# Low parts of the weights, the stages of sums, and the first norm's squares in another order: a decoder block on one core

## The chip, the core and the metric

One core of a Trainium2 chip runs the whole kernel. The metric is device microseconds of one execution, the median of repeated runs. In profiles the engines are PE (TensorE's matmuls), PEld (its weight loads), DVE (VectorE), ACT (ScalarE), POOL (GpSimd) and SP (SyncE, which here only issues the weights' loads and the stores of the result).

## The reference

A decoder block for 256 tokens of width 2048, one layer, all in float32:

```python
x = x + 0.5 * swiglu(rms_norm(x, ffn1_norm_g[l]), ffn1_w_gate[l], ffn1_w_up[l], ffn1_w_down[l])
h = rms_norm(x, mix_norm_g[l])
z = h @ w_in[l]
...
merged = jax.nn.sigmoid(gate_a) * attn_branch + jax.nn.sigmoid(gate_c) * conv_branch
x = x + merged @ w_out[l]
x = x + 0.5 * swiglu(rms_norm(x, ffn2_norm_g[l]), ffn2_w_gate[l], ffn2_w_up[l], ffn2_w_down[l])
return rms_norm(x, final_norm_g)
```

`swiglu` is `(silu(h @ w_gate) * (h @ w_up)) @ w_down` with 5632 columns between. Attention (8 heads, differential) and a causal convolution of width 31 over 1024 channels stand between the two feed-forward parts. The change touches how the matrix products are fed and emptied, and the mean of squares in the first `rms_norm`; what is computed stays the same.

## The kernel before

**Products in two parts.** Each float32 operand is the sum of a high part (rounded to the matmul's format, `wh` for a weight, the first 256 columns of `h`) and a low part (`wl`, the last 256 columns). A product is high x high, high x low and low x high. In `lin` (line 312) the weights stand still in TensorE: a *high* matmul streams the 512 columns of h against `wh`, a *low* one 256 columns against `wl`. A call of `lin` makes 512 columns of the result in four PSUM banks, one for each column tile; there are five such banks in the pool. It runs over units of four row tiles of 128 (`KU`), four units for 2048 rows. A unit has 16 high and 16 low matmuls, in the order high, low, or low, high in the odd units and the last one.

**Weights.** Class `Weights` (line 43) brings units of 1 MB from HBM, on SP's queue, into three raw buffers. ACT rounds a half of a unit (two row tiles, `KH`) to `wh` (`high_to`, line 89; L94), DVE subtracts to get `wl` (`low_to`, line 97; L103). There are six buffers for high halves and four for low ones; a raw buffer is loaded anew once its second low half is made. `next` (line 110) hands out a half, and first issues the high and low parts up to six and four halves ahead.

**The order of the work.** Every engine takes its instructions in the order in which the program issues them. There is no scheduler: `lin` calls `tick` (line 314) after a column tile of high matmuls or two of low ones, and each tick moves every open *flow* and the *side* jobs on. A flow is the emptying of one column tile (`evac`), a generator in stages. `halves_sum` (line 389) has ACT copy one half of the bank (rh, L392) and DVE add the other (L394). A gate product's sums go on to a product with rstd (L404), a silu on ACT (L406) and a product on POOL (L407); an up product's to a product with the gate (L424) and a split into high and low parts (L261 on ACT, L263 on DVE). `tick` takes the flows from the oldest to the newest.

**The first product.** x and the first weights arrive in pieces. For the first three units `lin` goes half by half (`halves`, line 329): `before` splits the next two tiles of x into parts of h (`split_x`, line 457; L256 on ACT, L258 on DVE), then `W.next(early=False)` issues low parts up to four halves ahead. `split_x` also squares its two tiles on POOL and adds them to `acc1` (L273, L275). After the first product `gate_late` runs `rstd_steps` in side ticks: a matmul with ones for the mean (L296), then a reciprocal root. The gate's sums wait for it in SBUF.

Of the kernel before, what the change touches and what calls it, by code (L numbers as in the profile page):

```python
# [9 lines left out]
F32 = mybir.dt.float32  # L10
F32R = mybir.dt.float32r
AF = mybir.ActivationFunctionType
ALU = mybir.AluOpType
AX = mybir.AxisListType

P = 128
T = 256
D = 2048
# [7 lines left out]
KU = 4  # L26
KH = 2
# [14 lines left out]
class Weights:  # L42
# [54 lines left out]
    def low_to(self, n):  # L97
        while self.nlow < min(n, len(self.units) * KU // KH):
# [6 lines left out]
            if k + KH == KU:  # L105
                del self.raw[u]
                self.load_to(u + 1 + self.raw_bufs)

    def next(self, held=0, early=True):


        i = self.i

        def ahead(bufs):
            n = i + bufs - held
            if self.extra and n > min(self.extra) and i <= max(self.extra):
                n = min(n + len(self.extra), max(self.extra) + 1 + bufs)
            return n

        if early:  # L120
            self.high_to(ahead(self.high_bufs))
        self.low_to(ahead(self.low_bufs))
        self.i += 1
        return self.highs.pop(i), self.lows.pop(i)

# [30 lines left out]
def block_kernel(  # L156
# [5 lines left out]
    nc = tc.nc  # L162

    const = ctx.enter_context(tc.tile_pool(name="const", bufs=1))
    big = ctx.enter_context(tc.tile_pool(name="big", bufs=1))
# [48 lines left out]
    W = Weights(nc, wpool, units, moving)  # L214
# [5 lines left out]
    xT = big.tile([P, KT, T], F32, name="xT")  # L220
# [44 lines left out]
    def tmp():  # L265
        return work.tile([P, T], F32, name="t", tag="t", bufs=5)

    def add_square(acc, src, first, square=None):
        dst = acc if first else tmp()
        if square is None:  # L270
            nc.scalar.activation(dst, src, AF.Square)
        else:
            square.tensor_tensor(dst, src, src, ALU.mult)  # L273
        if not first:
            nc.gpsimd.tensor_tensor(acc, acc, dst, ALU.add)  # L275

    def rsqrt(dst, src, scale, eps):

        shape = list(dst.shape)
        v = work.tile(shape, F32, name="rs_v", tag=f"rsv{shape[-1]}", bufs=1)  # L280
        t = tmp()[:, 0:shape[-1]]
        nc.vector.tensor_scalar(v, src, scale, eps, ALU.mult, ALU.add)
        nc.scalar.activation(dst, v, AF.Sqrt)
        yield
        nc.vector.reciprocal(dst, dst)
        yield
        nc.vector.tensor_tensor(t, dst, dst, ALU.mult)
        nc.vector.tensor_tensor(t, t, v, ALU.mult)
        yield
        nc.vector.tensor_scalar(t, t, -0.5, 1.5, ALU.mult, ALU.add)  # L290
        nc.vector.tensor_tensor(dst, dst, t, ALU.mult)
        yield

    def mean_d(acc):
        ps = pmisc.tile([P, CK], F32, name="ps_mean", tag="misc")
        nc.tensor.matmul(ps[:, 0:T], lhsT=ones, rhs=acc, start=True, stop=True)  # L296
        return ps[:, 0:T]
# [6 lines left out]
    def rstd_steps(acc, rstd, n, eps):  # L304
        yield from rsqrt(rstd, mean_d(acc), D / n, eps)
# [5 lines left out]
    side = Side()  # L311
    flows = []

    def tick(n=1):

        for f in list(flows):
            if next(f, flows) is flows:
                flows.remove(f)
        side.tick(n)

    def lin(nk, xs, evac, before=None):

        ps = [psum.tile([P, CK], F32, name="ps_mm", tag="mm") for _ in range(4)]
        nu = nk // KU

        def high(ct, parts, kt, i):
            w = parts[i // KH][0][:, i % KH, ct * P:(ct + 1) * P]  # L330
            nc.tensor.matmul(ps[ct], lhsT=w, rhs=xs(kt + i), start=(kt + i == 0), stop=(kt + i == nk - 1))  # L331

        def low(ct, parts, kt, i):
            w = parts[i // KH][1][:, i % KH, ct * P:(ct + 1) * P]
            nc.tensor.matmul(ps[ct][:, T:2 * T], lhsT=w, rhs=xs(kt + i)[:, 0:T], start=False, stop=False)  # L335

        def halves(u):

            for h in range(KU // KH):
                before(u * (KU // KH) + h)  # L340
                parts = [W.next(early=False)]
                for i in range(KH):
                    for ct in range(4):
                        high(ct, parts, u * KU + h * KH, i)
                for ct in range(4):
                    for i in range(KH):
                        low(ct, parts, u * KU + h * KH, i)
                tick(4)

        for u in range(nu):  # L350
            last = u == nu - 1
            if before is not None and not last:
                halves(u)
                continue
            parts = []
            for h in range(KU // KH):
                if before is not None:
                    before(u * (KU // KH) + h)
                parts.append(W.next(held=h))
            for product in ((low, high) if last or u % 2 == 1 else (high, low)):  # L360
                for ct in range(4):
                    for i in range(KU):
                        product(ct, parts, u * KU, i)
                    if product is high:
                        if last:
                            flows.append(evac(ct, ps[ct]))
                        tick(1.4)
                    elif ct % 2 == 1:
                        tick(1.2)
# [20 lines left out]
    def halves_sum(dst, ps, scale=1.0):  # L390
        r = work.tile([P, T], F32, name="rh", tag="rh", bufs=3)
        nc.scalar.activation(r, ps[:, T:2 * T], AF.Copy, scale=scale)  # L392
        if scale == 1.0:
            nc.vector.tensor_tensor(dst, ps[:, 0:T], r, ALU.add)  # L394
        else:
            nc.vector.scalar_tensor_tensor(dst, ps[:, 0:T], scale, r, ALU.mult, ALU.add)

    def ffn_up(h, rstd, grp, a, before=None, late=None):
        s_2 = None

        def pair_of(ci, s_t):
            def gate_act(ct):
                s = s_t[:, ct, :]
                nc.vector.tensor_tensor(s, s, rstd, ALU.mult)  # L404
                yield
                nc.scalar.activation(s, s, AF.Silu)  # L406
                nc.gpsimd.tensor_tensor(s, s, rstd, ALU.mult)  # L407

            def gate_evac(ct, ps):
                halves_sum(s_t[:, ct, :], ps)  # L410
                if late is None or ci > 0:
                    yield from gate_act(ct)
                else:
                    yield

            def gate_late():
                yield from late
                for ct in range(4):
                    yield from gate_act(ct)

            def up_evac(ct, ps):
                t = tmp()
                halves_sum(t, ps)
                nc.vector.tensor_tensor(t, t, s_t[:, ct, :], ALU.mult)  # L424
                yield
                yield from split(a(ci * 4 + ct), t)

            lin(KT, h, gate_evac, before if ci == 0 else None)
            if late is not None and ci == 0:
                side.add(gate_late(), 0.5)  # L430
            lin(KT, h, up_evac)

        for ci in range(len(grp)):
            if ci % 2 == 0:
                s_2 = big.tile([P, 2, 4, T], F32, name="s_t", tag="y")
            pair_of(ci, s_2[:, ci % 2])
# [19 lines left out]
    h1 = split_pair("P", "h1_")  # L456
    acc1, rstd1 = norm_tiles("1")

    def split_x(kt):

        fs = [split_scaled(h1(kt + k), xT[:, kt + k, :], g1_sb[:, kt + k:kt + k + 1]) for k in range(2)]
        for f in fs:
            next(f)
        for f in fs:
            next(f, None)
        for k in range(2):
            add_square(acc1, xT[:, kt + k, :], kt + k == 0, square=nc.gpsimd)

    def start(u):
        if u == 0:  # L470
            W.ahead = 1
            split_x(0)
            W.split_first()
        if u < 7:
            split_x(2 * u + 2)
        else:
            W.ahead = 3

    loads = {}

# [50 lines left out]
    for gi, grp in enumerate(groups):  # L531
        a = split_pair("Q", "a1_")
        if gi == 0:
            ffn_up(h1, rstd1, grp, a, start, rstd_steps(acc1, rstd1, D, 1e-6))
        else:
            ffn_up(h1, rstd1, grp, a)
        last = None
        if gi == len(groups) - 1:
            hm = split_pair("P", "hm_")
            accm, rstdm = norm_tiles("m")  # L540
            last = next_norm(hm, accm, loads["gm"])
        for dc in range(4):
            lin(len(grp) * 4, a, residual_evac(dc, 0.5, last))
# [376 lines left out]
    for gi, grp in enumerate(groups):  # L920
        a = split_pair("P", "a2_")
# [28 lines left out]
    for tt in range(2):  # L950
        v, y, r = ms[:, tt:tt + 1], yf[:, tt:tt + 1], rf[:, tt:tt + 1]
        for n, (c0, c1) in enumerate(((0, 512), (512, 1024), (1024, 1536), (1536, 1792), (1792, 2048))):
# [13 lines left out]
            sq = work.tile([P, CK], F32, name="sqf", tag="s2", bufs=1)  # L966
# [64 lines left out]
```

## Time and profile before

| | us |
|---|---|
| median of 3 runs (2100.57 to 2101.76) | 2100.95 |
| the profiled execution | 2100.18 |
| its span | 2098.4 |
| TensorE busy in the span | 2065.3 |

The span is the time between the first and the last instruction of the profiled execution; what lies around it is 1.8 us. A matmul's end is modelled, since matmuls overlap, so TensorE's idle time as the profile counts it begins a little late, and its rate is better read from the starts of blocks of matmuls in the chain.

### The profile page before, as it was taken

The page shows a single profiled execution, that of the slowest core. Times are in us where ns is not written, and L with a number is a line of the kernel's source. Part 1 is how long each engine was busy: PE and PEld are TensorE (multiplying, and loading weights), DVE is VectorE, ACT ScalarE, POOL GpSimd, SP SyncE. Part 2 cuts the span into 40 slices and gives each one's busy share as a digit, 9 for nine tenths or more (in the row PEclk, how much of TensorE's full clock was granted, in tenths as well). Part 3 has the DMA queues.
Part 4 walks back from the last instruction along what each step waited for, and adds up shares of the span by engine and source line. Part 5 has one row for each costly group of instructions (what it writes and reads, how often), then busy time and mean ns, then how long its engine had stood idle before and what let it go on. Part 6 is the DMA issues. An engine that isn't in the chain of part 4 may idle for free.

```text
span 2098.4 us, 28546 instructions
## 1 busy us (share of the span) xinstructions
PE 2065.3 (98%) x11230; PEld 1775.8 (85%) x11230; DVE 1375.9 (66%) x1915; ACT 1004.8 (48%) x1456; POOL 190.6 (9%) x227
## 2 busy tenths in 40 slices
PE   7999999999999999999999999999999999999998
PEld 6888888888888888888778888888888888888887
DVE  8565555665565785889888666665655655645565
ACT  6454344443344554445555744554443444434443
POOL 6201012110010110000000000100100001000011
PEclk9999999999999999999999999999999999999999
DMA  6645555566545545555545555554455555554553
GB/s 241 197 171 212 188 177 206 189 216 218 181 180 202 193 174 201 181 187 186 183 166 180 198 181 181 198 203 180 168 214 183 184 195 181 201 193 168 203 198 121
DMA packets 57735, 397.54 MB, mean 189 GB/s; under 512 B 6888, under 2 KB 6992, under 8 KB 10752
## 3 DMA queue, kind: packets, MB, share of 16 engines
q1 hardware_dynamic: 55872, 390.10, 52.2%
q0 software_dynamic: 1728, 5.61, 0.9%
q8 instruction: 88, 1.44, 0.3%
q14 instruction: 47, 0.39, 0.1%
HBM read 392.00 MB, written 3.68 MB: 189 GB/s over the span
## 4 chain that ended last, share of the span: by engine, by line
PE 88%; DVE 7%; ACT 2%; DMA 1%; issue 1%; SPq 0%; DVEq 0%; ACTq 0%
PE ps_mm L331 40%; PE ps_mm L335 21%; PE ps_mm L375 9%; PE ps_mm L376 9%; PE ps_mm L377 9%; DVE wl L103 3%; DVE t L394 2%; DVE t L424 1%; ACT rh L392 1%; DMA w<-in_ffn_w_gate_dram 1%; ACT a L261 1%; DMA w<-in_ffn_w_down_dram 1%; PE ps_s L718 0%; PE ps_o L763 0%; PE ps_tr L907 0%
## 5 line engine op out<-in xcount | busy, mean ns | idle before, releaser
L103 DVE TENSOR_TENSOR wl<-w,wh 128x1024 fp32r<-128x1024 f32 x731 | 883.3, 1248 | 484.2 <-ACT wh L94 239.9
L94 ACT ACTIVATE wh<-w 128x1024 fp32r<-128x1024 f32 x731 | 742.8, 1053 | 704.0 <-PE ps_mm L331 377.5
L331 PE MATMUL ps_mm<-h,wh 128*128 128x512 f32 x2816 | 665.2, 392 | 10.8 <-DVE h L258 10.8
L331 PEld LDWEIGHTS ps_mm<-h,wh 128*128 128x128 f32 x2816 | 523.0, 189 | 117.4 <-ACT wh L84 6.2
L335 PEld LDWEIGHTS ps_mm<-h,wl 128*128 128x128 f32 x2816 | 340.9, 188 | 25.4 <-DVE wl L103 18.1
L335 PE MATMUL ps_mm<-h,wl 128*128 128x256 f32 x2816 | 349.8, 279 | 11.2 <-DVE wl L103 11.2
L407 POOL TENSOR_TENSOR s_t<-s_t,rstd 128x256 f32<-128x256 f32 x88 | 82.7, 940 | 1158.8 <-ACT s_t L406 1158.8
L331 PE MATMUL ps_mm<-a,wh 128*128 128x512 f32 x704 | 164.9, 390 | 0.4 <-DVE t L394 0.4
L331 PEld LDWEIGHTS ps_mm<-a,wh 128*128 128x128 f32 x704 | 130.4, 188 | 26.9 <-DVE t L394 0.8
L392 ACT ACTIVATE rh<-ps_mm 128x256 f32<-128x256 f32 x208 | 77.3, 372 | 153.7 <-PE ps_mm L331 153.7
L375 PE MATMUL ps_mm<-wl,a 128*128 128x512 f32 (+1 forms) x344 | 133.1, 387 | 0.0
L377 PE MATMUL ps_mm<-wh,a 128*128 128x512 f32 (+1 forms) x344 | 132.1, 384 | 0.0
L376 PE MATMUL ps_mm<-wh,a 128*128 128x512 f32 (+1 forms) x344 | 131.9, 384 | 0.0
L375 PE MATMUL ps_mm<-wl,hm 128*128 128x512 f32 x320 | 129.8, 406 | 0.0
L377 PE MATMUL ps_mm<-wh,hm 128*128 128x512 f32 x320 | 125.1, 391 | 0.0
L376 PE MATMUL ps_mm<-wh,hm 128*128 128x512 f32 x320 | 124.9, 390 | 0.0
L331 PE MATMUL ps_mm<-hm,wh 128*128 128x512 f32 x512 | 121.0, 392 | 0.0
L331 PEld LDWEIGHTS ps_mm<-hm,wh 128*128 128x128 f32 x512 | 94.7, 188 | 19.1
L619 DVE SCALAR_TENSOR_TENSOR y_sb<-u_sb,cw_sb,y_sb 128x256 f32<-128x256 f32 x240 | 105.0, 478 | 0.0
L394 DVE TENSOR_TENSOR t<-ps_mm,rh 128x256 f32<-128x256 f32 x112 | 47.5, 424 | 63.1 <-ACT rh L392 62.9
L335 PEld LDWEIGHTS ps_mm<-a,wl 128*128 128x128 f32 x704 | 84.5, 188 | 4.5 <-DVE wl L103 2.7
L335 PE MATMUL ps_mm<-a,wl 128*128 128x256 f32 x704 | 85.6, 278 | 1.9 <-DVE wl L103 1.9
(194 smaller groups left out, 1708.2 us busy)
## 6 DMA issues: line engine op xcount, KB each, us to landing
w<-in_ffn_w_up_dram SPq DMA_DIRECT2D x88, 1024.0 KB, 4.9
w<-in_ffn_w_down_dram SPq DMA_DIRECT2D x88, 1024.0 KB, 4.9
w<-in_ffn_w_gate_dram SPq DMA_DIRECT2D x85, 1024.0 KB, 4.9
w<-in_w_in_dram SPq DMA_DIRECT2D x72, 1024.0 KB, 4.8
w<-in_w_out_dram SPq DMA_DIRECT2D x16, 1024.0 KB, 4.9
w<-in_w_attn_branch_dram SPq DMA_DIRECT2D x8, 1024.0 KB, 4.8
w<-in_w_conv_branch_dram SPq DMA_DIRECT2D x8, 1024.0 KB, 4.8
w<-in_ffn_w_gate_dram SPq DMA_DIRECT2D x5, 512.0 KB, 8.5
```

The costliest lines, as they stand in the source:

```text
L94: self.nc.scalar.activation(wh, self.raw[u][:, k:k + KH], AF.Copy)
L103: self.nc.vector.tensor_tensor(wl, self.raw[u][:, k:k + KH], self.highs[h].bitcast(F32), ALU.subtract)
L261: nc.scalar.activation(dst[:, 0:T], src, AF.Copy)
L331: nc.tensor.matmul(ps[ct], lhsT=w, rhs=xs(kt + i), start=(kt + i == 0), stop=(kt + i == nk - 1))
L335: nc.tensor.matmul(ps[ct][:, T:2 * T], lhsT=w, rhs=xs(kt + i)[:, 0:T], start=False, stop=False)
L375: nc.tensor.matmul(ps, lhsT=hi, rhs=wl[:, kk, :], start=(first and kk == 0), stop=False)
L376: nc.tensor.matmul(ps, lhsT=hi, rhs=wh[:, kk, :], start=False, stop=False)
L377: nc.tensor.matmul(ps, lhsT=lo, rhs=wh[:, kk, :], start=False, stop=(last and kk == KH - 1))
L392: nc.scalar.activation(r, ps[:, T:2 * T], AF.Copy, scale=scale)
L394: nc.vector.tensor_tensor(dst, ps[:, 0:T], r, ALU.add)
L407: nc.gpsimd.tensor_tensor(s, s, rstd, ALU.mult)
L619: nc.vector.scalar_tensor_tensor(y, src, w, y, ALU.mult, ALU.add)
```

## The change

Four edits. (1) In the last and the odd units, where the low matmuls come first, `more_lows` issues one further low half before the unit's high matmuls and a second one before the third of their four column tiles, where `next` issued both at the start of the following unit. (2) `tick` takes the flows from the newest to the oldest. (3) In the first product's halves the low parts run two halves ahead in place of four (and with them the high parts that they need). (4) The squares leave POOL: a side job `squares`, from the 27th tick on, squares four tiles at a time on ACT and adds them up on DVE; the mean waits for it (`rstd_first`). `W.ahead` was set but never read.

```diff
--- before.py
+++ after.py
@@ -106,6 +106,10 @@
                 del self.raw[u]
                 self.load_to(u + 1 + self.raw_bufs)
 
+    def more_lows(self, n):
+
+        self.low_to(self.i + self.low_bufs - KU // KH + n)
+
     def next(self, held=0, early=True):
 
 
@@ -119,7 +123,9 @@
 
         if early:
             self.high_to(ahead(self.high_bufs))
-        self.low_to(ahead(self.low_bufs))
+            self.low_to(ahead(self.low_bufs))
+        else:
+            self.low_to(i + 2)
         self.i += 1
         return self.highs.pop(i), self.lows.pop(i)
 
@@ -313,7 +319,8 @@
 
     def tick(n=1):
 
-        for f in list(flows):
+
+        for f in flows[::-1]:
             if next(f, flows) is flows:
                 flows.remove(f)
         side.tick(n)
@@ -357,8 +364,13 @@
                 if before is not None:
                     before(u * (KU // KH) + h)
                 parts.append(W.next(held=h))
-            for product in ((low, high) if last or u % 2 == 1 else (high, low)):
+            order = (low, high) if last or u % 2 == 1 else (high, low)
+            for product in order:
+                if product is high and order[0] is low:
+                    W.more_lows(1)
                 for ct in range(4):
+                    if product is high and order[0] is low and ct == 2:
+                        W.more_lows(2)
                     for i in range(KU):
                         product(ct, parts, u * KU, i)
                     if product is high:
@@ -463,18 +475,38 @@
             next(f)
         for f in fs:
             next(f, None)
-        for k in range(2):
-            add_square(acc1, xT[:, kt + k, :], kt + k == 0, square=nc.gpsimd)
 
     def start(u):
         if u == 0:
-            W.ahead = 1
             split_x(0)
             W.split_first()
         if u < 7:
             split_x(2 * u + 2)
-        else:
-            W.ahead = 3
+
+    squared = []
+
+    def squares():
+
+        sq = big.tile([P, 4, 4 * T], F32, name="sq", tag="sgc")
+        for i in range(4):
+            nc.scalar.activation(sq[:, i].rearrange("p (k t) -> p k t", k=4), xT[:, 4 * i:4 * i + 4, :], AF.Square)
+            yield
+            if i % 2 == 1:
+                nc.vector.tensor_tensor(sq[:, i - 1], sq[:, i - 1], sq[:, i], ALU.add)
+                yield
+        nc.vector.tensor_tensor(sq[:, 0], sq[:, 0], sq[:, 2], ALU.add)
+        yield
+        nc.vector.tensor_tensor(sq[:, 0, 0:2 * T], sq[:, 0, 0:2 * T], sq[:, 0, 2 * T:4 * T], ALU.add)
+        yield
+        nc.vector.tensor_tensor(acc1, sq[:, 0, 0:T], sq[:, 0, T:2 * T], ALU.add)
+        squared.append(True)
+
+    def rstd_first():
+        while not squared:
+            yield
+        yield from rstd_steps(acc1, rstd1, D, 1e-6)
+
+    side.add(squares(), 1.0, delay=26)
 
     loads = {}
 
@@ -531,7 +563,7 @@
     for gi, grp in enumerate(groups):
         a = split_pair("Q", "a1_")
         if gi == 0:
-            ffn_up(h1, rstd1, grp, a, start, rstd_steps(acc1, rstd1, D, 1e-6))
+            ffn_up(h1, rstd1, grp, a, start, rstd_first())
         else:
             ffn_up(h1, rstd1, grp, a)
         last = None
```

The order shows it in three places. The first is DVE at the end of a gate product, the second one of the kernel (s_t holds the gate's sums; wl is a low half). Before:

```order
L103 TENSOR_TENSOR wl<-w,wh 128x1024 x6
L394 TENSOR_TENSOR s_t<-ps_mm,rh 128x256
L404 TENSOR_TENSOR s_t<-s_t,rstd_113 128x256
L394 TENSOR_TENSOR s_t<-ps_mm,rh 128x256
L404 TENSOR_TENSOR s_t<-s_t,rstd_113 128x256
L394 TENSOR_TENSOR s_t<-ps_mm,rh 128x256
L404 TENSOR_TENSOR s_t<-s_t,rstd_113 128x256
L394 TENSOR_TENSOR s_t<-ps_mm,rh 128x256
L404 TENSOR_TENSOR s_t<-s_t,rstd_113 128x256
L103 TENSOR_TENSOR wl<-w,wh 128x1024 x8
```

With the change (lines shift by 12 here):

```order
L103 TENSOR_TENSOR wl<-w,wh 128x1024 x7
L406 TENSOR_TENSOR s_t<-ps_mm,rh 128x256
L416 TENSOR_TENSOR s_t<-s_t,rstd_113 128x256
L406 TENSOR_TENSOR s_t<-ps_mm,rh 128x256
L416 TENSOR_TENSOR s_t<-s_t,rstd_113 128x256
L103 TENSOR_TENSOR wl<-w,wh 128x1024
L406 TENSOR_TENSOR s_t<-ps_mm,rh 128x256
L416 TENSOR_TENSOR s_t<-s_t,rstd_113 128x256
L406 TENSOR_TENSOR s_t<-ps_mm,rh 128x256
L416 TENSOR_TENSOR s_t<-s_t,rstd_113 128x256
L103 TENSOR_TENSOR wl<-w,wh 128x1024 x7
```

One of the low halves that stood behind the four sums now stands ahead of the first, one ahead of the third.

The second is DVE in the first product (h are the parts of x, sq the squares, acc their sum). Before:

```order
L258 SCALAR_TENSOR_TENSOR h_0_110<-xT,g_sb,h_0_110 128x256 x2
L103 TENSOR_TENSOR wl<-w,wh 128x1024 x3
L258 SCALAR_TENSOR_TENSOR h_0_110<-xT,g_sb,h_0_110 128x256 x2
L103 TENSOR_TENSOR wl<-w,wh 128x1024
...
L103 TENSOR_TENSOR wl<-w,wh 128x1024
L394 TENSOR_TENSOR s_t<-ps_mm,rh 128x256 x4
L103 TENSOR_TENSOR wl<-w,wh 128x1024 x2
L282 TENSOR_SCALAR rs_v<-ps_mean 128x256
```

With the change:

```order
L264 SCALAR_TENSOR_TENSOR h_0_110<-xT,g_sb,h_0_110 128x256 x2
L103 TENSOR_TENSOR wl<-w,wh 128x1024
L264 SCALAR_TENSOR_TENSOR h_0_110<-xT,g_sb,h_0_110 128x256 x2
L103 TENSOR_TENSOR wl<-w,wh 128x1024
...
L406 TENSOR_TENSOR s_t<-ps_mm,rh 128x256 x2
L495 TENSOR_TENSOR sq<-sq 128x1024
L103 TENSOR_TENSOR wl<-w,wh 128x1024
L406 TENSOR_TENSOR s_t<-ps_mm,rh 128x256 x2
L495 TENSOR_TENSOR sq<-sq 128x1024
L497 TENSOR_TENSOR sq<-sq 128x1024
L499 TENSOR_TENSOR sq<-sq 128x512
L501 TENSOR_TENSOR acc_112<-sq 128x256
```

The h parts of the third half no longer stand behind three low halves, and the additions of the squares, with a low half among them, now stand between the first product's sums and the mean. On TensorE the matmul for the mean moves from 8 to 12 high matmuls into the second product. The third place is ACT, from the end of an up product (rh and the split into `a`) on. Before:

```order
L392 ACTIVATE rh<-ps_mm 128x256
L261 ACTIVATE a_0_116<-t 128x256
L392 ACTIVATE rh<-ps_mm 128x256
L261 ACTIVATE a_0_116<-t 128x256
L392 ACTIVATE rh<-ps_mm 128x256
L261 ACTIVATE a_0_116<-t 128x256
L392 ACTIVATE rh<-ps_mm 128x256
L94 ACTIVATE wh<-w 128x1024 x2
L261 ACTIVATE a_0_116<-t 128x256
```

With the change:

```order
L404 ACTIVATE rh<-ps_mm 128x256 x2
L267 ACTIVATE a_0_116<-t 128x256
L404 ACTIVATE rh<-ps_mm 128x256
L267 ACTIVATE a_0_116<-t 128x256
L404 ACTIVATE rh<-ps_mm 128x256
L267 ACTIVATE a_0_116<-t 128x256
L94 ACTIVATE wh<-w 128x1024 x2
L267 ACTIVATE a_0_116<-t 128x256
```

Each rh now stands ahead of the split of the tile before it. SP's order is the same as before; POOL's loses the 31 operations on squares, and nothing else of it moves against TensorE's work.

## Rows read from the trace of the kernel before

**Rows 1.** The page, busy time of each engine over the whole span.
```profile
PE 2065.3 (98%) x11230; PEld 1775.8 (85%) x11230; DVE 1375.9 (66%) x1915; ACT 1004.8 (48%) x1456; POOL 190.6 (9%) x227
```

**Rows 2.** Waits of TensorE, whole span: us in total, times, longest.
```profile
PE ps_mm L335 <- DVE wl L103: 13.9, 41, 0.6
PE ps_mm L331 <- DVE h L258: 10.8, 4, 5.8
PE ps_mm L331 <- DVE t L394: 0.4, 1, 0.4
```

**Rows 3.** The chain in order of time: start us, us, what.
```profile
39.75 0.43 PE ps_mean L296 x2
...
42.03 3.63 PE ps_mm L335 x32
...
68.34 7.28 PE ps_mm L331 x32
...
158.40 7.28 PE ps_mm L331 x32
...
225.28 7.28 PE ps_mm L331 x32
...
247.15 7.28 PE ps_mm L331 x32
```

**Rows 4.** Timeline at an up product's end: start us, us, instruction, [idle before].
```profile
56.43 7.44 PE L331 MATMUL ps_mm<-h,wh 128*128 128x512 f32 x32
...
61.46 0.42 DVE L394 TENSOR_TENSOR t<-ps_mm,rh 128x256 f32<-128x256 f32 x1 [0.42 <-ACT rh L392]
...
63.70 0.42 DVE L424 TENSOR_TENSOR t<-t,s_t 128x256 f32<-128x256 f32 x1
63.71 2.23 PE L335 MATMUL ps_mm<-h,wl 128*128 128x256 f32 x18
64.04 2.35 DVE L103 TENSOR_TENSOR wl<-w,wh 128x1024 fp32r<-128x1024 f32 x2
...
66.45 1.90 PE L335 MATMUL ps_mm<-h,wl 128*128 128x256 f32 x14 [0.51 <-DVE wl L103]
```

**Rows 5.** Timeline of the first product.
```profile
12.10 1.06 ACT L94 ACTIVATE wh<-w 128x1024 fp32r<-128x1024 f32 x1 [2.19 <-DMA w<-in_ffn_w_gate_dram]
...
16.75 1.69 DVE L258 SCALAR_TENSOR_TENSOR h<-xT,g_sb,h 128x256 fp32r<-128x256 f32 x2
...
17.63 3.78 PE L331 MATMUL ps_mm<-h,wh 128*128 128x512 f32 x8 [4.46 <-DVE h L258]
...
21.56 1.06 ACT L94 ACTIVATE wh<-w 128x1024 fp32r<-128x1024 f32 x1 [1.97 <-DMA w<-in_ffn_w_gate_dram]
...
34.69 5.06 PE L331 MATMUL ps_mm<-h,wh 128*128 128x512 f32 x21 [0.25 <-DVE h L258]
```

**Rows 6.** Windows: stretch, length, PE, PEld, DVE, ACT, POOL busy, PEclk, DMA, GB/s.
```profile
17.63:22.85 5.22, 5.22 (x16) 4.45 (x17) 5.22 (x5) 3.25 (x6) 5.06 (x6) 0.51 0.92 388
22.86:25.80 2.94, 2.94 (x19) 2.62 (x18) 2.94 (x4) 2.94 (x6) 2.78 (x4) 1.00 0.49 137
```

**Rows 7.** Durations of single kinds of instruction: by source line, timeline, costliest groups.
```profile
L258 DVE SCALAR_TENSOR_TENSOR hm<-xT,gm_sb,hm x16: 473/480/962, 703.5 to 758.7; 128x256 fp32r<-128x256 f32 x16
...
L645 ACT ACTIVATE u_sb<-y_sb x2: 1042/1044/1046, 1158.0 to 1158.9; 128x1024 f32<-128x1024 f32 x2
...
1160.01 1.23 DVE L624 TENSOR_TENSOR u_sb<-u_sb 128x1024 f32<-128x1024 f32 x1 [3.99 <-ACT u_sb L645]
...
1162.28 0.68 DVE L626 TENSOR_TENSOR u_sb<-u_sb 128x512 f32<-128x512 f32 x1
...
26.03 0.89 ACT L256 ACTIVATE h<-xT,g_sb 128x256 fp32r<-128x256 f32 x2
...
28.05 1.76 DVE L103 TENSOR_TENSOR wl<-w,wh 128x1024 fp32r<-128x1024 f32 x1
...
L619 DVE SCALAR_TENSOR_TENSOR y_sb<-u_sb,cw_sb,y_sb 128x256 f32<-128x256 f32 x240 | 105.0, 478 | 0.0
```

## The prediction

> **What bounds the kernel now.** I read the page's busy line first: TensorE is busy 98% of 2098.4 us, no other engine over 66% [rows 1]. So an edit on another engine pays only where TensorE waits for it. The waits of TensorE, read next, name three places [rows 2]: 41 waits for a low part of a weight (DVE, L103), four for h (DVE, L258), one for a sum that frees a PSUM bank (DVE, L394). Those idle times start at the modelled end of the matmul before, so they are too short; I take the cost from the chain in order of time. There a matrix product without a wait takes 21.87 us (225.28 to 247.15), and two pairs of gate and up products with four waits take 90.06 us (68.34 to 158.40) [rows 3]. Four free ones are 87.48, so a wait costs 2.58 / 4 = 0.645 us.
>
> The timeline shows how such a wait is made [rows 4]. The last 16 high matmuls of the up product start at about 56.5 (the first half of the 32; the other half is the next product's). Four column tiles are summed, one after the other: rh on ACT, sum and product on DVE, split on ACT, and the next rh stands behind that split. The third sum ends at 61.88, 5.4 us after the start, and the last product at 64.12. Only then does DVE reach the two low parts, until 66.39. TensorE has used up its ready ones at 65.7 and goes on at 66.45.
>
> The start is the second place [rows 5]. DVE stands at the low parts of weight halves 1 to 3, whose loads come late, and the low parts of h tiles 4 and 5 are behind them (16.75). TensorE waits 4.46 us until 17.63. Then its granted clock is 0.51, the lower level of 1.2 GHz, for 16 matmuls that take 5.22 us [rows 6]; at 2.4 GHz they take 8 x (0.2275 + 0.1143) = 2.74 (a half of 64 + 64 in 21.87 us, the high matmul twice the low one), so the slow clock costs 2.5 more.
>
> **Part 1: low parts earlier, newest sum first.** The instructions stay the same in number; DVE's order moves. One low part of the next product now stands ahead of the first sum, one ahead of the third. Laid on the same product end (t = 0 at the first of the 16 high matmuls): DVE ends the two lows queued before at about 0.7, the new one at 1.9 (1.18 each, from the pair of 2.35 [rows 4]); two tiles of 0.85 (two operations of 0.42) end at 3.6, the second new low at 4.8, the third sum at 5.2. ACT does not hold this up: rh of the next tile now stands ahead of the split of the one before. So both lows are there at 4.8, and TensorE asks for them at 3.65 + 3.65 + 1.83 = 9.1. The wait goes: 41 x 0.645 = **26.4 us**. The wait of 0.4 for a PSUM bank goes too, as the sums no longer wait in turn for splits: 0.5 with the restart. What is late next? The fourth column tile of the next product takes the bank of the third sum at 3.65 + 3 x 0.91 = 6.4; the sum ends at 5.2. That margin of 1.2 us is the cover; under the convolution, with one more operation of 0.48 in each tile [rows 7], it shrinks to about 0.5, and nothing of it is lost in my sum. Raw weight buffers come free earlier, so SP's loads start earlier; its order is unchanged.
>
> **Part 2: start, halves first.** Each half of the first product now asks for one low part ahead, not three, and 31 POOL operations are gone. TensorE's third half then waits only for its high part: landed 12.10, plus 1.06 [rows 5], so 13.2 in place of 17.63, no stop, and no slow clock. From there a half costs 2.74 on TensorE, and DVE needs 1.2 + 2 x 0.48 = 2.2 [rows 4, 7]. These are rows with a quiet POOL; beside POOL's squares the same operations took 1.76 and 0.85 [rows 5, 7], 3.45 a half, more than TensorE needs. The Trainium skill, SBUF — State Buffer, section Who interferes with whom, says that a VectorE operation with two SBUF inputs blocks with a GpSimd one that reads SBUF. By that rule the quick values hold here; if the slowness had another cause the start would be some 4 us worse (six halves of 3.45 less 2.74).
>
> The sixth half ends at 24.1. The last four tiles of weights land at 21.56 [rows 5], and then follow, on ACT, a high part (1.06), two h (0.89 [rows 7]), a high part (1.0), and on DVE, behind the low parts of those two h, the weight's low part: about 26.0. TensorE stops at 24.4 for **1.7 us**. 14 low and 16 high matmuls later, at 31.4, the first product is done; before it was 34.69 + 5.06 less 8 matmuls of the next (1.82), 37.9. So 6.5 us are gained up to here.
>
> **Part 3: squares.** POOL's 16 squares and 15 sums go; ACT gets four of 1.04, DVE three sums of 1.23, one of 0.68, and one of 256 elements, as long as L424's 0.42 [rows 4, 7]. This is not hidden. The mean's matmul stands 12 matmuls into the second product, so TensorE is there at 31.4 + 2.73 = 34.1. But on ACT each square stands between two rh (rh from 28.9, second square done 31.6, last 34.1), and DVE runs: a low part to 29.6, two sums, the first addition (waits for the second square) to 32.8, another low part to 34.0, two sums to 34.8, then 1.23 + 1.23 + 0.68 + 0.42. Acc is there at 38.3, and TensorE waits **4.1 us**. All matmuls behind the mean wait with it; on DVE the reciprocal and the low parts of the third unit stand behind it, which TensorE asks for 3.65 + 7.28 = 10.9 us later, so nothing more is lost there. With 0.43 for the mean and four matmuls (0.91) the first high block ends at 39.6; before, at 42.03 [rows 3]. That is a gain of 2.4, if the clock holds. A wait of 4.1 is nearest to the row of 4.46, after which it fell, so I take the fall, priced at its 2.5. The start nets **+0.1**; the bounds are -2.4, and about +2.6 with a fall after the 1.7 us stop too.
>
> **Sum.** The profiled execution took 2100.18 us (span 2098.4 and 1.8 around it). 2100.18 - 26.4 - 0.5 + 0.1 = 2073.4. The median of three runs, 2100.95, is 0.8 above it: **2074 us**.
>
> **Rivals.** *A, the waits shrink but stay.* DVE is later at the product's end than I laid out, and the third sum misses 6.4 by a few tenths: a wait for the PSUM bank takes the place of half of the gain. For it: DVE is the releaser in every wait now; against: a margin of 1.2. Half of 26.4: about 2087.
>
> *B, slower.* The new low part is queued ahead of the sums, and it cannot start before TensorE has ended the low matmuls whose buffer it takes. If the two lows push the third sum back by their full 2.35, with nothing won by the new order of the sums, it ends at 5.4 + 2.35 = 7.75, and TensorE waits 1.35 at the fourth tile of the next product. That decides from a shift of 1.0 us on. 44 gate and up products x 1.35 = 59, less 26.9: 2133. Against: rows 4 show that DVE waits for rh 0.42 in each tile, which is the time that the low part would fill.
>
> *C, the start wins nothing or loses.* The waits of parts 2 and 3 come out longer, or both are followed by the slow clock: 2074 + 2.5 to 5, so 2077 to 2079. The Trainium skill, TensorE: Matmul & The Clock Gate, section on HAM oscillation, says that bursts parted by waits pay the slow clock anew each time; by that rule alone C's lower figure would be the forecast. The row of 4.46 agrees; of shorter stops the trace says only that one of 0.25 (at 34.69) left the next 21 matmuls at full speed.
>
> *D, the start wins more.* The squares come earlier than laid out, or the clock holds: 2069 to 2072.
>
> **Chances.** Forecast 0.5, C 0.15, D 0.15, A 0.12, B 0.05, and 0.03 that the waits only change their releaser and the time stays. The range 2068 to 2083 holds the first four cases but most of A and leaves out B. Measurements of this kernel tell 0.2%, 4.2 us, from no change. Faster by more: 0.92; within: 0.03; slower: 0.05.
>
> **What would show it.** Right: TensorE's 41 waits for L103 nearly gone and gate and up pairs at 43.8 in the chain; a stop before the mean of about 4 us with acc's DVE sum as releaser, and a granted clock near 0.5 after it; DVE's h parts at 0.48 in the first 30 us. Wrong: waits for L394 or L441 at the fourth tile of a product (A, B), or a first high block of the second product that ends outside 37 to 45.

## The result, and the profile after

The changed kernel takes 2072.5 us (median, 2072.41 to 2072.7), before 2101.34 in the same job: a ratio of 0.9863, 95% interval 0.9846 to 0.9880. The forecast was 2074 in a range of 2068 to 2083.

The page's busy line after, as in [rows 1]:

```profile
PE 2052.3 (99%) x11230; PEld 1772.3 (86%) x11230; DVE 1358.1 (66%) x1920; ACT 1020.9 (49%) x1460; POOL 170.3 (8%) x196
```

The matmuls are the same in number, and no engine but TensorE was near its limit; the span fell by 27.5 us (2098.4 to 2070.9), and what went is TensorE standing or starting anew. The waits of TensorE, as in [rows 2] (us in total, times, longest):

```profile
PE ps_mm L338 <- ACT wh L84: 5.6, 1, 5.6
PE ps_mean L302 <- DVE acc L501: 4.0, 1, 4.0
PE ps_mm L342 <- DVE wl L103: 1.0, 1, 1.0
```

The 41 waits for a low part, those for h inside the first product and the one for a PSUM bank are gone. The first line is the kernel's start. Before, it was the longest of the four waits for h in [rows 2], 5.8 us, so only three of those four were stops inside the work. The other two lines are new stops, both in the first 40 us. The chain in order of time, against [rows 3], shows both sides (start us, us, what):

```profile
38.71 1.19 PE ps_mean L302 x2
39.90 1.71 PE ps_mm L338 x4
41.61 5.15 PE ps_mm L342 x32
...
46.76 7.28 PE ps_mm L338 x32
...
68.63 7.28 PE ps_mm L338 x32
...
156.10 4.10 PE ps_mm L338 x18
```

From 68.63 on, two pairs of products take 87.47 us, where they took 90.06: four products at the free 21.87. But the 32 low matmuls from 41.61 on take 5.15 us, where the same block took 3.63. So the second unit of the second product begins at 46.76; before it was 42.03 + 3.63 = 45.66. At that point **the changed kernel is 1.1 us behind**. From there to the end it takes 2024.1 us against 2052.7: **28.6 us gained**.

Where the 28.6 come from is seen in the timeline at the end of the same up product as in [rows 4] (start us, us, instruction):

```profile
55.75 3.50 DVE L103 TENSOR_TENSOR wl<-w,wh 128x1024 fp32r<-128x1024 f32 x3 [3.01 <-ACT wh L94]
...
57.53 7.44 PE L338 MATMUL ps_mm<-h,wh 128*128 128x512 f32 x32
...
60.90 1.22 DVE L103 TENSOR_TENSOR wl<-w,wh 128x1024 fp32r<-128x1024 f32 x1
...
62.03 0.42 DVE L406 TENSOR_TENSOR t<-ps_mm,rh 128x256 f32<-128x256 f32 x1
...
64.81 3.82 PE L342 MATMUL ps_mm<-h,wl 128*128 128x256 f32 x32
```

The block of high matmuls starts at 57.70 by the chain. The second new low half is there at 62.12 and the third sum at 62.45, that is 4.4 and 4.75 us later; before, the third sum came 5.4 us after the block's start and the low halves 9.9. TensorE asks for the last two low halves at 64.81 + 1.83 = 66.6 and has them 4.5 us early. Its 32 low matmuls now stand in one row.

The start, against [rows 5]:

```profile
13.87 1.98 PE L338 MATMUL ps_mm<-h,wh 128*128 128x512 f32 x8
...
16.76 0.87 DVE L264 SCALAR_TENSOR_TENSOR h<-xT,g_sb,h 128x256 fp32r<-128x256 f32 x2
...
17.55 1.22 DVE L103 TENSOR_TENSOR wl<-w,wh 128x1024 fp32r<-128x1024 f32 x1
...
26.36 1.93 PE L342 MATMUL ps_mm<-h,wl 128*128 128x256 f32 x14 [0.98 <-DVE wl L103]
...
28.12 6.57 PE L338 MATMUL ps_mm<-h,wh 128*128 128x512 f32 x28
...
33.10 1.22 DVE L103 TENSOR_TENSOR wl<-w,wh 128x1024 fp32r<-128x1024 f32 x1
...
36.15 1.23 DVE L497 TENSOR_TENSOR sq<-sq 128x1024 f32<-128x1024 f32 x1
...
38.14 0.42 DVE L501 TENSOR_TENSOR acc<-sq 128x256 f32<-128x256 f32 x1
...
38.71 1.19 PE L302 MATMUL ps_mean<-acc,ones 128*128 128x256 f32 x2 [4.02 <-DVE acc L501]
```

The third half starts at 13.87 in place of 17.63, and 16 of the 28 high matmuls from 28.12 end the first product at 31.8 in place of 37.9. Then TensorE stands for 4.02 us before the mean. The windows give the clock there (stretch, length, busy time of PE, PEld, DVE, ACT, POOL, PEclk, DMA share, GB/s):

```profile
28.12:34.69 6.57, 6.57 (x30) 5.07 (x28) 5.25 (x8) 6.57 (x11) 0.00 (x0) 1.00 0.72 301
34.69:38.71 4.02, 0.00 (x1) 0.03 (x1) 3.77 (x5) 2.85 (x3) 0.00 (x0) 0.90 0.73 261
38.71:41.40 2.69, 2.69 (x6) 2.14 (x7) 0.98 (x2) 1.00 (x2) 0.00 (x0) 0.50 0.00 0
41.40:44.00 2.60, 2.60 (x14) 2.59 (x13) 1.20 (x1) 2.58 (x3) 0.00 (x0) 0.50 0.00 0
44.00:46.76 2.76, 2.76 (x22) 2.76 (x22) 2.12 (x2) 0.10 (x1) 0.00 (x0) 0.87 0.00 0
```

After the stop the granted clock is 0.50, the lower level (1.2 GHz). From 38.71 to 46.76 are 8.05 us for a mean of 0.43, four high matmuls (0.91) and 32 low ones (3.66): 5.0 at 2.4 GHz, so the slow clock costs 3.05. The windows say when it was slow: 0.90 over the 4.02 us of the stop puts the fall 0.8 us before TensorE goes on, at 37.9, and 0.87 in the last window puts the rise at 44.7. So TensorE works 6.0 us at half the clock and loses half of that. After the stop of 0.98 at 25.4 the clock was 1.00.

### The profile page after: what moved, and what is told of

Its sections match the earlier page's. It is cut to its first block, busy times and chain, and to the rows that moved or that the text cites. A ratio compares the mean times of both kernels' runs of the same rounds, so it can differ in the third digit from the quotient of the medians.

```text
span 2070.9 us, 28539 instructions
## 1 busy us (share of the span) xinstructions
PE 2052.3 (99%) x11230; PEld 1772.3 (86%) x11230; DVE 1358.1 (66%) x1920; ACT 1020.9 (49%) x1460; POOL 170.3 (8%) x196
## 4 chain that ended last, share of the span: by engine, by line
PE 98%; DMA 1%; DVE 1%; ACT 0%; issue 0%; SPq 0%; ACTq 0%; DVEq 0%
PE ps_mm L338 46%; PE ps_mm L342 23%; PE ps_mm L387 9%; PE ps_mm L388 9%; PE ps_mm L389 9%; DMA w<-in_ffn_w_gate_dram 1%; PE ps_s L750 0%; PE ps_o L795 0%; DVE wl L103 0%; PE ps_mg L903 0%; PE ps_tr L939 0%; ACT wh L94 0%; PE ps_mean L302 0%; PE ps_at L785 0%; DVE sq L495 0%
## 5 line engine op out<-in xcount | busy, mean ns | idle before, releaser
L342 PE MATMUL ps_mm<-h,wl 128*128 128x256 f32 x2816 | 340.3, 278 | 1.0 <-DVE wl L103 1.0
L419 POOL TENSOR_TENSOR s_t<-s_t,rstd 128x256 f32<-128x256 f32 x88 | 88.9, 1020 | 1162.2 <-ACT s_t L418 1162.2
L338 PEld LDWEIGHTS ps_mm<-a,wh 128*128 128x128 f32 x704 | 130.4, 188 | 26.1
L389 PEld LDWEIGHTS ps_mm<-wh,a 128*128 128x128 f32 x344 | 64.5, 187 | 13.9
```

What stands on the lines that cost most here:

```text
L389: nc.tensor.matmul(ps, lhsT=lo, rhs=wh[:, kk, :], start=False, stop=(last and kk == KH - 1))
```

## The experiments

The theory had three parts to test: that edits 1 and 2 bring all of the gain and the start nothing; that POOL's squares are what made DVE slow in the start; and that the stop at the mean, with the clock behind it, takes back what edits 3 and 4 won. The rivals stand in the expectations.

**Edits 1 and 2 without the start.** `more_lows` and the reversed `tick` on the kernel before.

```diff
-        for f in list(flows):
+        for f in flows[::-1]:
...
+                if product is high and order[0] is low:
+                    W.more_lows(1)
                 for ct in range(4):
+                    if product is high and order[0] is low and ct == 2:
+                        W.more_lows(2)
```

> Edits 1 and 2 alone on the kernel before; the start stays as it was. Theory (the prediction's part 1): the whole gain lies behind the first 46 us, where the two traces differ by 28.6 us, and the start edits are worth nothing or a small loss. Then this kernel takes 2101.3 - 28.6 = 2072.7 us, its first low block of the second product starts at 42.0 as before, and the waits of TensorE for low parts are gone. Rival: the start edits brought part of the gain, by a DVE that enters the steady state earlier: then it takes over 2076 and waits for low parts stay.

Measured 2071.57 us (ratio 0.9858, 0.9842 to 0.9875). TensorE's only waits are those of the start:

```profile
PE ps_mm L334 <- ACT wh L84: 5.9, 1, 5.9
PE ps_mm L334 <- DVE h L261: 5.2, 3, 3.8
```

The theory holds: the whole gain is in these two edits, and the change with its start is 0.9 us slower than they are alone. Their second unit's high block in the second product starts at 45.39 in the timeline, the change's at 46.60 (46.76 in the chain).

**Edits 3 and 4 alone.** The change's diff without `more_lows`, and with `list(flows)`.

```diff
+        else:
+            self.low_to(i + 2)
...
-        for k in range(2):
-            add_square(acc1, xT[:, kt + k, :], kt + k == 0, square=nc.gpsimd)
...
+    side.add(squares(), 1.0, delay=26)
...
-            ffn_up(h1, rstd1, grp, a, start, rstd_steps(acc1, rstd1, D, 1e-6))
+            ffn_up(h1, rstd1, grp, a, start, rstd_first())
```

> Edits 3 and 4 alone (halves two ahead, squares on ACT and DVE). Theory: the start ends 1.1 us later than before, as in the changed kernel (46.76 against 45.66 for the second unit's block), and the 41 waits stay: 2101.3 + 1.1 = 2102.4 us. By the prediction's own term of +0.1 it would be 2101.4. Rival: the start edits are worth more than 2 us by themselves: under 2099.

Measured 2103.22 us (1.0010, 1.0001 to 1.0019): a small loss, as the theory has it, of 1.9 us where 1.1 was expected; the interval, 0.2 to 4.0 us, holds both.

```profile
PE ps_mm L342 <- DVE wl L103: 14.9, 42, 1.0
...
PE ps_mean L302 <- DVE acc L497: 5.5, 1, 5.5
```

The waits for low parts are all there, and the stop at the mean is 5.5 us, not 4.0. DVE's timeline shows why the stop is longer:

```profile
33.96 2.35 DVE L103 TENSOR_TENSOR wl<-w,wh 128x1024 fp32r<-128x1024 f32 x2
...
39.47 0.42 DVE L497 TENSOR_TENSOR acc<-sq 128x256 f32<-128x256 f32 x1
```

Without `more_lows` two low halves stand together among the additions, where the change has one (33.10 above), and acc is ready at 39.89 in place of 38.56.

**Edit 2 alone, edit 1 alone.** Each on the kernel before; the first is the one line of `tick` above, the second the `more_lows` lines.

> Edit 2 alone on the kernel before (newest sum first, low parts still behind all four sums). Theory (each of the three waits of 0.42 us that DVE had for rh in a product's end is gone): DVE reaches the two low parts 1.26 us earlier, so the second of them ends at 65.1 instead of 66.39, before TensorE asks for it at 65.7: the waits go for the plain products too, 2073 to 2078 us, and edit 1 is then only a margin. Rival (the place of the low parts decides): most of the 41 waits stay at 0.2 us or more: 2085 to 2095.

> Edit 1 alone on the kernel before (more low parts ahead, sums still oldest first, so each rh still stands behind the split before it). Theory (the low parts were late, and one ahead of the sums cures it): the waits for low parts go, but the sums have lost the room that edit 2 gave them: by the prediction's laying out, the third sum moves from 5.4 to 5.4 + 1.2 (one low part ahead of it, the 0.42 us waits for rh taking up some) = 6.0 to 6.6 us after the product's last high block begins, against 6.4 at which TensorE takes its bank: 44 waits of 0 to 0.3 us, 2073 to 2085 us. Rival B of the prediction, in this kernel: both low parts push the third sum to 7.75, 44 x 1.35 = 59 us more, over 2120.

Edit 2 alone: 2072.26 us (0.9866, 0.9851 to 0.9880). Edit 1 alone: 2074.55 (0.9876, 0.9862 to 0.9891). The waits of TensorE, edit 2 alone, then edit 1 alone:

```profile
PE ps_mm L331 <- DVE h L258: 10.6, 3, 5.9
...
PE ps_mm L334 <- DVE h L261: 10.9, 3, 5.8
PE ps_mm L334 <- DVE xT L450: 0.7, 3, 0.3
```

No wait for a low part is left in either. These two kernels ran in another job than both edits together, and the kernel before took 2100.35 us in this job and 2101.35 in that one, so the traces compare them better. From the second unit's high block in the second product (45.49 before, 45.39 with both edits, 46.05 with edit 2, 45.85 with edit 1) to the end of the span, the kernels take 2052.9, 2024.3, 2025.0 and 2026.9 us. Both edits gain 28.6 us there, edit 2 alone 28.0, edit 1 alone 26.1. **Either of them brings over nine tenths of the gain by itself.**

Before, DVE waited for rh at three of the four sums by 0.76, 0.42 and 0.42 us; [rows 4] has the second, and these are the other two:

```profile
59.75 0.42 DVE L394 TENSOR_TENSOR t<-ps_mm,rh 128x256 f32<-128x256 f32 x1 [0.76 <-ACT rh L392]
...
63.17 0.42 DVE L394 TENSOR_TENSOR t<-ps_mm,rh 128x256 f32<-128x256 f32 x1 [0.42 <-ACT rh L392]
```

The timeline of edit 2 alone, at the same product's end:

```profile
56.98 7.44 PE L331 MATMUL ps_mm<-h,wh 128*128 128x512 f32 x32
...
62.75 2.35 DVE L103 TENSOR_TENSOR wl<-w,wh 128x1024 fp32r<-128x1024 f32 x2
...
64.26 3.82 PE L335 MATMUL ps_mm<-h,wl 128*128 128x256 f32 x32
```

The low halves still stand behind all four sums, but DVE no longer waits for rh between tiles and begins them 5.8 us after the block's start, in place of 7.6. It ends them at 65.10, and TensorE asks for them at 64.26 + 1.83 = 66.09: they are 1.0 us early, where before they were 0.7 late. With edit 1 alone DVE does wait for rh, while TensorE has its low parts in time; what is late is the sum:

```profile
60.37 0.42 DVE L402 TENSOR_TENSOR t<-ps_mm,rh 128x256 f32<-128x256 f32 x1 [0.76 <-ACT rh L400]
...
62.71 0.42 DVE L402 TENSOR_TENSOR t<-ps_mm,rh 128x256 f32<-128x256 f32 x1
...
63.18 0.76 PEld L334 LDWEIGHTS ps_mm<-h,wh 128*128 128x128 f32 x4 [0.29 <-DVE t L402]
```

The third sum ends at 63.13 and TensorE's weight loads stand 0.29 us for its bank. That is the mechanism of the prediction's rivals A and B, at a fraction of its price; in the whole trace it shows as weight loads held up four times, by 0.4 us at most.

**Edit 3 alone, edit 4 alone.** Edit 3 is the `else: self.low_to(i + 2)` on the kernel before, with POOL's squares; edit 4 is `squares` and `rstd_first` with low parts four halves ahead.

> Edit 3 alone on the kernel before: low parts two halves ahead in the first product, squares still on POOL. Theory (POOL's squares slow DVE's operations with two SBUF inputs, 1.75 against 1.23 us for a low part, 0.85 against 0.48 for a low part of h): no stop of 4.46 us before the third half, but a half takes DVE 1.75 + 1.71 = 3.46 us against TensorE's 2.74, so the sixth starts at about 24.5 instead of 22.2, and POOL's last addition, at 37.6 as before, holds up the mean for 1 to 2 us: 2099 to 2102. Rival (the slow DVE operations had another cause, the traffic of the loads): DVE's operations are at 1.23 and 0.48 although POOL squares.

> Edit 4 alone on the kernel before: squares on ACT and DVE, low parts of the first product still four halves ahead. Theory (the stop before the third half comes from DVE's order, and edit 3 alone removes it): that stop stays at about 4 us, with the slow clock behind it, DVE's operations are quick (1.23, 0.48), and the stop at the mean comes on top with its own slow clock: 2101.3 + 5 to 7 = 2106 to 2108. Rival (quick DVE operations alone cure the stop): under 2103.

Edit 3 alone: 2101.44 us (1.0003, 0.9994 to 1.0013), no difference. Edit 4 alone: 2105.91 (1.0027, 1.0017 to 1.0036), slower. The same two operations of DVE in both, first beside POOL's squares (edit 3 alone):

```profile
18.29 1.71 DVE L260 SCALAR_TENSOR_TENSOR h<-xT,g_sb,h 128x256 fp32r<-128x256 f32 x2
19.92 1.76 DVE L103 TENSOR_TENSOR wl<-w,wh 128x1024 fp32r<-128x1024 f32 x1
...
28.21 0.50 PE L337 MATMUL ps_mm<-h,wl 128*128 128x256 f32 x2 [2.08 <-DVE wl L103]
31.38 3.35 PE L337 MATMUL ps_mm<-h,wl 128*128 128x256 f32 x14 [2.67 <-DVE wl L103]
```

then with POOL quiet (edit 4 alone):

```profile
17.11 3.66 PE L331 MATMUL ps_mm<-h,wh 128*128 128x512 f32 x8 [3.37 <-DVE h L258]
...
18.51 0.88 DVE L258 SCALAR_TENSOR_TENSOR h<-xT,g_sb,h 128x256 fp32r<-128x256 f32 x2
19.30 1.22 DVE L103 TENSOR_TENSOR wl<-w,wh 128x1024 fp32r<-128x1024 f32 x1
...
43.32 1.19 PE L296 MATMUL ps_mean<-acc,ones 128*128 128x256 f32 x2 [5.09 <-DVE acc L492]
```

POOL's squares are the cause: 1.76 against 1.22 and 0.85 against 0.44 each. Edits 3 and 4 together, which differ from edit 3 alone by the squares only, have 1.22 and 0.44 as well. Traffic is not the cause: the loads were as busy in both, 348 GB/s beside POOL's squares and 376 without, up to 24 us. The Trainium skill, SBUF — State Buffer, section Who interferes with whom, says that a VectorE operation with two SBUF inputs contends with a GpSimd one that reads SBUF; these rows agree. Neither edit alone cures the start. With edit 3 alone DVE is the bound and TensorE waits 2.08 and 2.67 us at the first product's end, with the clock at 0.50 from within the second of them, in place of the stop before the mean that I expected. With edit 4 alone the old stop stays (3.37) and the mean's (5.09) comes on top, each with the slow clock behind it.

**The mean later.** Three kernels move the mean's matmul in the changed kernel, by the rate and delay of one side job: 0.6 and 4 put it behind 8 low matmuls, 0.75 and 6 behind 16, 0.75 and 8 behind 32. The last of them:

```diff
-                side.add(gate_late(), 0.5)
+                side.add(gate_late(), 0.75, delay=8)
```

> The changed kernel with the mean's matmul 36 matmuls later (behind the 32 low ones of the second product's first unit). TensorE would reach it at 31.8 + 3.64 + 3.66 = 39.1, acc is there at 38.6. Theory (the stop at the mean and the slow clock behind it are what the start still loses): no stop, granted clock 1.00 throughout, 2072.5 - 4.2 - 3.0 = 2065.3 us. Rival: the low parts that stand behind the additions on DVE, or the reciprocal root that is now later, make a new wait before the end of the second product: 2068 or more, with that wait in the trace.

> The same with the mean's matmul behind the first 16 low ones: TensorE reaches it at 31.8 + 3.64 + 1.83 = 37.3 and waits 1.4 us for acc. Theory A (the clock falls after a stop of several us only; after the stop of 0.98 at 25 us it stayed at 1.00): 2065.3 + 1.4 = 2066.7 us at full clock. Theory B (any stop over 1 us costs the slow clock): 2066.7 + 3.0 = 2069.7.

> The changed kernel with the mean's matmul behind the first 8 low ones of the second product: TensorE reaches it at 31.8 + 3.64 + 0.91 = 36.4 and waits about 2.2 us for acc at 38.6. Measured so far: after stops of 0.98 to 1.16 us the granted clock stayed at 1.00, after stops of 3.37 us and more it fell to 0.50. If it holds here: 2066.1 + 2.2 = 2068.3 us; if it falls, 3.0 more: 2071.3.

| mean behind, in the second product | stop | granted clock after it | median us | ratio, interval |
|---|---|---|---|---|
| 12 high (the change) | 4.02 | 0.50 | 2072.50 | 0.9863, 0.9846 to 0.9880 |
| 16 high, 8 low | 1.89 | 0.50 in the profiled run | 2068.05 (2067.58 to 2069.59) | 0.9845, 0.9830 to 0.9860 |
| 16 high, 16 low | 0.99 | 1.00 | 2067.09 | 0.9837, 0.9822 to 0.9852 |
| 16 high, 32 low | none | 1.00 | **2066.06** | 0.9832, 0.9817 to 0.9846 |

With the mean behind 32 low matmuls the two windows that cost the change its start have TensorE busy throughout at full clock:

```profile
28.00:38.71 10.71, 10.71 (x61) 9.11 (x60) 9.29 (x13) 10.50 (x15) 0.00 (x0) 1.00 0.75 281
38.71:46.76 8.05, 8.05 (x41) 6.84 (x40) 7.91 (x11) 4.46 (x5) 0.00 (x0) 1.00 0.41 133
```

So the stop and the clock behind it are what the start lost: 6.4 us are back in the median, of 7.2 expected. In the timelines the high block after the first product's last low matmuls starts at 28.23 here and 28.12 in the change, the second unit's at 39.80 and 46.60: 11.57 us in place of 18.48, or 6.9 less. The spans differ by 6.5: 0.1 of the 6.9 went at a later start and 0.3 behind that second block's start. No wait in the list took the place of the stop. This kernel beats the change and edits 1 and 2 alone. Behind 8 low matmuls the profiled execution (2069.59 us) shows the fall:

```profile
38.00:39.00 1.00, 0.56 (x3) 0.54 (x4) 0.29 (x1) 0.00 (x0) 0.00 (x0) 1.00 0.20 82
...
40.00:41.00 1.00, 1.00 (x6) 1.00 (x6) 0.94 (x1) 1.00 (x3) 0.00 (x0) 0.50 0.00 0
```

Its three other runs took 2067.58 to 2068.44, about what the expectation gives for a clock that holds. No trace shows them, but their mean granted clock over the whole run was 0.999 in each, as in every run of the kernels behind 16 and 32, against 0.998 in the profiled run. So it most likely held in them.

**The late mean with one of edits 1 and 2.** The kernel with the mean behind 32, less `more_lows`, and less the reversed `tick`.

> Mean behind 32 low matmuls, edits 2, 3 and 4, without edit 1. Theory (edit 2 alone frees DVE early enough, edit 1 is a margin): the 41 waits stay away; two low halves stand ahead of acc on DVE where one did, so acc comes at about 39.7 against TensorE at 39.5: 2066.1 + 0 to 0.6 = 2066.1 to 2066.7 us. Rival (edit 1 is needed once the start is tight): waits for low parts, over 2068.

> Mean behind 32 low matmuls, edits 1, 3 and 4, without edit 2. Theory (edit 1 alone takes away the 41 waits, but leaves small waits for sums in the products before and after the mixer, 2.3 us more than both edits together): 2066.1 + 2.3 = 2068.4 us. Rival (with the quick start these small waits go as well): 2066.1.

Without edit 1: 2066.67 us (0.9838, 0.9823 to 0.9852), with a stop of 0.62 at the mean: as the theory has it. Without edit 2: 2069.28 (0.9848, 0.9832 to 0.9864), 3.2 more than with both, for 2.3 expected. (The 2.3 is the difference between edit 1 alone and edit 2 alone, not both together.) Its waits after the start:

```profile
PE ps_mm L338 <- DVE t L406: 1.7, 2, 0.9
...
PE ps_mm L338 <- DVE xT L454: 0.8, 3, 0.3
```

These five, 2.5 us in all, are for sums that come late; the two of 0.9 do not stand in edit 1 alone, so the small waits did not go with the quick start, as the rival had it, and two came new. Both kernels ran in a job where the kernel before was 0.7 us faster than in that of the late mean (2100.63 against 2101.35). So edit 1 can be spared at 0.6 to 1.3 us, and edit 2 at 3.2 to 3.9, with or without that 0.7.

## Why the prediction was right, and where its terms were off

**Part 1 was right in its mechanism and 6% too small.** Behind the first 46 us the change gains 28.6 us; the sum had 26.4 for the 41 waits and 0.5 for the PSUM bank. The term that was mis-sized is the 0.645 a wait: it came from four waits in two pairs; over all 41, taken as equal, it is (28.6 - 0.5) / 41 = 0.69. The margin behind it held: the third sum was laid out at 5.2 and came at 4.75, against 6.4. The laying out, though, put edits 1 and 2 into one account. The runs show that each alone takes all 41 waits away, so "one low half ahead of the sums" was not needed for the 26.4, and neither was "newest first"; but edit 1 without edit 2 makes sums late, and gives back 2.5 us of the 28.6.

**Part 2 was right.** No stop before the third half, DVE's operations at the quick values, a product that ends at 31.8 for 31.4 laid out (the third half started at 13.87 for 13.2, since its high part began at 12.59 for 12.10), and a stop for the late weights of 0.98 for 1.7.

**Part 3 was right on the stop and short on the clock.** TensorE reached the mean at 34.69 for 34.1, acc came at 38.56 for 38.3, and it waited 4.02 for 4.1 (by its own terms, 38.3 less 34.1, 4.2). "Priced at its 2.5" is the term that was mis-sized: the slow clock cost 3.05. The price was taken from one row as if it were fixed. In [rows 6], 0.51 over 5.22 us is 5.1 us of work at half the clock, which costs 2.6; here it is 6.0 us, which costs 3.0. Other runs show less: behind the stop of 3.75 with edits 1 and 2 alone the clock is 0.56 over 3.5 us, a cost of 1.5, and behind the 3.37 of edit 4 alone 0.56 over 3.9, a cost of 1.7. What sets when the clock rises again no run here shows. With the product's end 0.4 late this makes the start +1.1 for +0.1.

**The sum.** Against the profiled span: -27.5 for -26.8. The two errors, 1.7 more gain and 1.0 more loss, partly cancel, so by luck the total is closer than either part.

**The rivals.** A and B did not come; B's place, the fourth column tile, shows waits of 0.3 to 0.9 behind the start only where edit 2 is missing. C was right in its direction, 1.0 us of its 2.5, and D's cause did not come, though the time ended 0.5 us from its 2072. The rule behind C, in the Trainium skill, TensorE: Matmul & The Clock Gate, section HAM oscillation, is that bursts parted by waits pay the slow clock anew. The page says it of waits as long as those of its own example, a condition that the prediction left out when it counted the 1.7 us stop. Here the stops of 0.98, 0.99 and 1.16 us did not pay it, those of 3.37 us and more did, and so did the two of 2.08 and 2.67 with two matmuls between them; one of 1.89 did in its profiled run.

What the forecast did not see: edits 3 and 4 are worth 5.5 us (2071.57 to 2066.06) once the mean's matmul stands 36 matmuls later (no run has one of the two alone with the late mean). The 4.1 us were laid out as the price of the squares; they were the price of a place.

## What to carry to other kernels

When an in-order engine is late by a little, look at its own short waits inside the stretch first: waits of 0.76, 0.42 and 0.42 us for rh at a product's end were enough for 41 waits of about 0.69 on TensorE, and turning the order of a loop took them away without moving the late work itself. Where a result is needed late (here the root of the mean, by the end of the product), put the instruction that waits for it behind work that is ready, because an in-order engine that reaches it early stops everything queued behind it and, where the stop is long, as the 4.02 us here, pays for the clock as well. Test edits that serve one goal one at a time: two that are each enough look like one that is needed.

## What the hardware did that I had not expected

- The price of the slow clock does not follow the length of the stop: a stop of 4.02 us was followed by a loss of 3.05, one of 4.46 by 2.5, one of 3.75 by 1.5, while a stop of 0.99 in nearly the same place as the first cost nothing more. Taking the stop of 4.02 away was worth 6.4 us in the median.
- POOL and DVE slowed each other: with edit 3 alone one and the same 128x256 product took POOL 1.60 us at 31.88, beside DVE's low parts, and 0.61 at 35.11, while DVE stood.
- The column of the granted clock does not tell all at the kernel's start. It reads 1.00 there, but the first eight high matmuls, at 5.64, took 3.78 us, as long as the eight at 17.63 in [rows 5], under 0.51 in [rows 6]; the eight at 13.87 took 1.98.
